# Layer 1's gate summed beside the layer's first products, and the squares of retention's output on ScalarE

## The chip, the cores and the metric

The kernel runs on one core of one Trainium2 chip. The metric is the device time of one execution in microseconds. Three executions of the kernel before took 675.12, 677.21 and 678.33 us; the median is 677.21. A core has TensorE (PE in the profile, its weight loads PEld), VectorE (DVE), ScalarE (ACT), GpSimd (POOL) and SyncE (SP, which here issues the transfers). Each works through its own list of instructions in order; semaphores make one wait for another.

## The reference

A trunk of two layers on 512 tokens of width 1024, in float32. In each layer

```
mod = silu(c) @ w_ada[l] + b_ada[l];  shift, scale, gate = split(mod, 3)
h = rms_norm(x, norm_g[l]) * (1 + scale) + shift
proj = h @ w_in[l]                  # 1024 x 3712: q, k, v, gate of A, B and C
A: differential attention, 4 heads   B: dilated window attention, 6 heads x 3 patterns
C: retention in both directions, 4 heads, values of 96, then rms_norm over the 96
y = concat([oa, ob, oc] * silu of their gates) @ w_out[l]
x = x + gate * y
```

The gate is a row of 1024 numbers that is wanted only where x is updated, at the end of the layer. shift and scale are wanted at its start.

## The kernel before

Tokens lie in four tiles of 128 partitions (t = 0 to 3). Each float32 product is made of three matmuls on values split into a high and a low part: high by high, high by low, low by high (`products`, L322 to L333). A weight block is a `Piece`: SP loads 2 x 128 rows of it into one of the five buffers `raw`, ScalarE writes the high part (whi, wsp or wrow), VectorE or, for each third piece, GpSimd the low part (L302). A buffer of raw is free when both have read it.

The work of a layer is a list of groups of matmuls. `at(g, fn)` hangs a piece of other work on the number g of a group, and `issue` emits the groups in order, each followed by what hangs on it. A scheduler of the framework then orders each engine's instructions by its own estimates and places the waits. So the number in `at` sets roughly where work stands in each engine's list, and the emitted order of each engine is fixed before the run.

The layer boundary: at the end of layer 0 the output products of the second 512 columns run, token tile by token tile. For each tile VectorE forms y (L1112, product by gate) and x (L1117), ScalarE the sum of squares of x (junk), VectorE and GpSimd the factor of the norm (rstd, L1084, L569, L199) and the modulated tiles hn (`h_tile`; VectorE multiplies, GpSimd adds at L565), TensorE transposes four of them (L554), ScalarE writes the high part hT and VectorE the low part hL (L559). Right behind layer 0's output products TensorE begins layer 1's V columns, tile by tile, which need hT and hL of that tile, and then the Q columns.

The gate: `ada_steps` (L440 to L466) sums a half of it, 512 columns, in four steps. Each loads two rows of w_ada per partition, 512 KB, into a raw buffer, and adds them with two vector instructions (L459, through the helper at L159) into the accumulator ada_acc, one of two buffers that GpSimd clears and SP fills with the bias. Its end is a matmul with ones and a copy by ScalarE. `plan_ada` (L1070) hangs loads, additions and end on groups: a load six groups ahead of its additions, a step every four groups. Both halves are hung relative to g_gb, the group at which the last columns of B start: additions at g_gb - 55 and g_gb - 31 onward, ends at g_gb - 18 and g_gb - 17. In layer 1, g_gb is 128 groups behind g_v, the first group of V.

Retention C: `att` forms the scores, `chunk` (L952) sums inner and cross part of a token tile in PSUM, ScalarE copies them to cno, GpSimd squares them into csq (L960), VectorE sums the squares (css, L962), `rms_end` ends with a power on GpSimd (L199). `norm` (five groups later) multiplies on VectorE and GpSimd, `gate_done` comes later. csq lies in the pool "e" of five buffers, which the scores use too.

Of the kernel before, what the change touches and what calls it, by code (L numbers as in the profile page):

```python
# [9 lines left out]
F32 = mybir.dt.float32  # L10
F32R = mybir.dt.float32r
AF = mybir.ActivationFunctionType
OP = mybir.AluOpType
AX = mybir.AxisListType
PSUM = bass.MemoryType.PSUM

D = 1024
S = 512
L = 2
P = 128  # L20
# [5 lines left out]
H_C, DK_C, DV_C = 4, 48, 96  # L26
# [14 lines left out]
MODS = 12  # L41
H_0, H_1 = 8, 9
C_GAP, C_DECAY, C_TURN, C_STATE = 3, 4, 4, 7
C_ATT, C_PAIR, C_OUT, C_STEP, C_NORM = 8, 3, 13, 2, 7
GATE, GATE_GAP, GATE_END = 55, 24, 18
GB_OUT, PIECE_0, PIECE_M = 9, 2, 3              
SETUP, TABLES, RET_T, TAB1 = 12, 12, 19, 9      
N_A1, N_B1, N_SOFT = 5, 5, 9
# [81 lines left out]
def dram(ap, offset, dims):  # L130
    return bass.AP(tensor=ap.tensor, offset=ap.offset + offset, ap=[list(d) for d in dims])
# [3 lines left out]
def encoder(ctx, tc, x, c, norm_g, w_ada, b_ada, w_in, w_out, params, consts, out):  # L135
# [8 lines left out]
    ep = pool("ep", 5)  # L144
# [7 lines left out]
    V, A, G, T = nc.vector, nc.scalar, nc.gpsimd, nc.tensor  # L152
    dma = nc.sync.dma_start

    def act(o, i, f=AF.Copy, **kw):
        A.activation(o, i, f, **kw)  # L156

    def stt(o, a, s, b, op0, op1):
        V.scalar_tensor_tensor(o, a, s, b, op0, op1)  # L159
# [4 lines left out]
    def at(g, fn, *args):  # L164
        plan.setdefault(g, []).append((fn, args))
# [139 lines left out]
    def rows2(raw, w, first, row, pair, step, cnt, n):  # L305

        if cnt == 1:
            dma(raw[:, :, :n], dram(w, first, [[row, P], [pair, 2], [1, n]]))
            return
        for i in range(2):  # L310
            dma(raw[:, i, :cnt * n].rearrange("p (j n) -> p j n", j=cnt), dram(w, first + i * pair, [[row, P], [step, cnt], [1, n]]))
# [26 lines left out]
    def tok_(t):  # L338
        return slice(t * P, (t + 1) * P)
# [100 lines left out]
    def ada_steps(l, cols, use):  # L440

        (c0, n), cnt = cols[0], len(cols)
        step = cols[1][0] - c0 if cnt > 1 else 0
        z = {}

        def load(r):
            def fn():
                raw = z[r] = rp.tile([P, 2, 512], F32, name="raw")
                rows2(raw, w_ada, l * D * 3 * D + r * 3 * D + c0, KD * 3 * D, 3 * D, step, cnt, n)
                if r == 0:  # L450
                    a = z["a"] = two.tile([P, 512], F32, name="ada_acc")
                    G.memset(a, 0.0)
                    dma(a[0:1].rearrange("o (j n) -> o j n", j=cnt), dram(b_ada, l * 3 * D + c0, [[0, 1], [step, cnt], [1, n]]))
            return fn

        def add(r):
            def fn():
                for rr in range(2):
                    stt(z["a"], z[r][:, rr], cs[:, r + rr:r + rr + 1], z["a"], OP.mult, OP.add)  # L459
            return fn  # L460

        def end():
            ps = sc_p.tile([P, 512], F32, name="ada_ps", tag="sc")
            T.matmul(ps, ones, z["a"], start=True, stop=True)  # L464
            use(ps)
        return [load(r) for r in range(0, KD, 2)], [add(r) for r in range(0, KD, 2)], end  # L466
# [101 lines left out]
    def rms_end(s, n, width):  # L568
        V.tensor_scalar(s, s, 1.0 / width, EPS, OP.mult, OP.add)  # L569
        pow_half(s, s, n)  # L570
# [261 lines left out]
    class Retention:  # L832
# [41 lines left out]
        def qk_done(self, t, ps, g0):  # L874
            if t == 0:
                self.raw = {}
            raw = self.raw[t] = ep.tile([P, 8, DK_C], F32, name="craw", tag="e")
            act(raw.rearrange("p h n -> p (h n)"), ps[:, :384])
            g = g0 + 12 + C_GAP * t
            at(g + 1, self.rope, t)  # L880
            at(g + C_DECAY, self.decay, t)
            at(g + C_TURN, self.turn_qk, t)
            at(g + C_TURN + 1, self.turn_f, t)
            at(g + C_STATE, self.state, t)
            if t == NT - 1:
                at(g + C_ATT, self.back)
                for h in range(0, H_C, 2):
                    at(g + C_ATT + C_PAIR * h // 2, self.att, h)
                for n in range(NT):
                    at(g + C_OUT + C_STEP * n, self.chunk, n)  # L890
                    at(g + C_OUT + C_NORM + C_STEP * n, self.norm, n)

        def rope(self, t):
# [45 lines left out]

        def att(self, h):  # L940
            if h == 0:
                self.atts, self.o, self.ss = {}, {}, {}

            ps = [sc_p.tile([P, NT, P], F32, name="catt", tag="sc") for _ in range(2)]
            for n in range(NT):
                for j, r in enumerate((F_, B_)):
                    T.matmul(ps[j][:, n], self.qkT[r, 2 + h // 2, tok_(n)], self.qkT[r, h // 2, tok_(n)], start=True, stop=True)
            for j in range(2):
                at_ = self.atts[h + j] = ep.tile([P, NT, P], F32, name="att", tag="e")
                V.tensor_tensor(at_, ps[j], self.dcm[:, h + j].unsqueeze(1).to_broadcast([P, NT, P]), OP.mult)  # L950

        def chunk(self, n):  # L952
            ps = pv_p.tile([P, H_C, DV_C], F32, name="co", tag="pv")
            for h in range(H_C):
                T.matmul(ps[:, h], self.atts[h][:, n], self.vc[n][:, h], start=True, stop=False)
                T.matmul(ps[:, h], self.qfT[:, h, tok_(n)], self.st[n][:, h], start=False, stop=True)
            o = self.o[n] = one.tile([P, H_C, DV_C], F32, name=f"cno{n}", tag=f"s{4 + n}")
            act(o, ps)
            sq = ep.tile([P, H_C, DV_C], F32, name="csq", tag="e")
            G.tensor_tensor(sq, o, o, OP.mult)  # L960
            ss = self.ss[n] = sm.tile([P, H_C], F32, name="css")
            V.tensor_reduce(ss, sq, AX.X, OP.add)  # L962
            rms_end(ss, H_C, DV_C)

        def norm(self, n):
# [19 lines left out]
    def layer(l):  # L985
# [3 lines left out]
        if l:  # L989
            g_v, _ = in_chunk(l, [(COL_VC, 384)], ret.v_done, first=True)  # L990
# [36 lines left out]
        g_gb = len(groups)  # L1027
# [36 lines left out]
        def gate_use(hf):  # L1064
            def use(ps):
                z[hf] = two.tile([P, 512], F32, name="gate", tag="ga")
                act(z[hf], ps)
            return use

        def plan_ada(steps, g, gap, g_end=0):  # L1070
            loads, adds, end = steps
            for i in range(4):
                at(g + gap * i - 6, loads[i])
                at(g + gap * i, adds[i])
            at(max(g + gap * 4, g_end), end)
            return g + gap * 4

        for hf in range(2):
            plan_ada(ada_steps(l, [(2 * D + hf * 512, 512)], gate_use(hf)), g_gb - GATE + GATE_GAP * hf, 4, g_gb - GATE_END + hf)


        def h_stats(t):
# [15 lines left out]
        for hf in range(2):  # L1098
# [59 lines left out]
            for j, t in turns:  # L1158
# [9 lines left out]
                g = len(groups) - 1  # L1168
# [9 lines left out]
        if not last:  # L1178
            g = g_gb - MODS
            for q in range(4):  # L1180
                g = plan_ada(mod_steps(l + 1, q), g, 3)
# [76 lines left out]
    for l in range(1, L):  # L1258
        layer(l)
# [35 lines left out]
```

## Time and profile before

| | us |
|---|---|
| median of three runs | 677.21 |
| the profiled execution | 676.71 |
| its span | 674.9 |
| TensorE busy | 630.2 (93%) |
| VectorE busy | 501.0 (74%) |
| ScalarE busy | 330.4 (49%) |
| GpSimd busy | 261.4 (39%) |

The span runs from the first to the last recorded instruction of the core. Busy time is the time in which an engine executes; weight loads are counted apart from matmuls and overlap them. A time in brackets behind an instruction is the idle time of its engine ahead of it, with the work that ended it. Layer 0 ends, and layer 1 begins, at about 355 us. Layer 1's V columns end at about 380, its C part runs from about 430, its two attentions from about 460 to 600, its output products in the last 75 us.

### The profile page before, as it was taken

The numbers are of one execution on the slowest core, as the hardware profiler recorded it, in microseconds if no ns is written. First come the engines' busy times: TensorE is split into PE (matmuls) and PEld (weight loads), VectorE is DVE, ScalarE is ACT, GpSimd is POOL, SyncE is SP. The second block draws the span as 40 slices with busy tenths as digits, with TensorE's granted clock in tenths as the row PEclk, the third lists the DMA queues.
The fourth block names the chain that finished last, engine by engine and source line by source line (L and its number), as shares of the span: only waits on it lengthen the run. The fifth ranks groups of instructions, "written<-read, shape, count | busy, mean of one in ns | idle before, by whom it ended". The sixth has DMA issues, their size and how long they took to land.

```text
span 674.9 us, 10503 instructions
## 1 busy us (share of the span) xinstructions
PE 630.2 (93%) x3487; PEld 516.0 (76%) x3487; DVE 501.0 (74%) x1157; ACT 330.4 (49%) x722; POOL 261.4 (39%) x252
## 2 busy tenths in 40 slices
PE   6889998999999996999998999989999999989997
PEld 2778787977887784677776998887778887767786
DVE  1998697589988988897769154768997888576443
ACT  5534352447655674554423243434757476656410
POOL 3427363666343520211457252767052613121200
PEclk9789998999999999899999999999999999999999
DMA  9796133344555556575643122235454625423211
GB/s 316 250 335 159 57 94 97 105 120 120 148 127 173 144 165 170 166 243 181 216 166 119 32 83 75 64 84 155 114 156 119 193 85 161 116 64 133 93 63 63
DMA packets 87134, 93.20 MB, mean 138 GB/s; under 512 B 7044, under 2 KB 68004, under 8 KB 87080
## 3 DMA queue, kind: packets, MB, share of 16 engines
q1 hardware_dynamic: 87080, 92.53, 45.6%
q8 instruction: 28, 0.46, 0.3%
q14 instruction: 26, 0.21, 0.1%
HBM read 72.58 MB, written 4.19 MB: 114 GB/s over the span
## 4 chain that ended last, share of the span: by engine, by line
PE 41%; DVE 8%; POOL 4%; issue 2%; ACT 2%; DMA 0%; POOLq 0%; ACTq 0%; DVEq 0%; SPq 0%
PE acc L333 8%; PE acc L332 8%; PE acc L331 8%; PE tr L554 5%; PE pv L703 3%; PE acc L327 1%; PE acc L329 1%; PE acc L328 1%; DVE wlo L302 1%; PE sc L726 1%; PE sc L787 1%; DVE ada_acc L159 1%; PE sc L788 1%; DVE pt L693 1%; PE ada_ps L464 1%
## 5 line engine op out<-in xcount | busy, mean ns | idle before, releaser
L331 PE MATMUL acc<-whi,hT 128*128 128x384 f32 (+1 forms) x424 | 155.4, 366 | 1.5 <-ACT vc L156 1.0
L333 PE MATMUL acc<-whi,hL 128*128 128x384 f32 (+1 forms) x424 | 153.2, 361 | 0.0
L332 PE MATMUL acc<-wlo,hT 128*128 128x384 f32 (+1 forms) x424 | 152.7, 360 | 0.0
L302 POOL TENSOR_TENSOR wlo<-raw,whi 128x768 fp32r<-128x768 f32 (+1 forms) x26 | 55.1, 2119 | 126.4 <-ACT whi L156 119.2
L156 ACT ACTIVATE whi<-raw 128x768 fp32r<-128x768 f32 (+1 forms) x75 | 69.6, 929 | 52.9 <-PE acc L333 41.6
L331 PEld LDWEIGHTS acc<-whi,hT 128*128 128x128 f32 x424 | 80.2, 189 | 8.5 <-ACT vc L156 1.4
L302 DVE TENSOR_TENSOR wlo<-raw,whi 128x384 fp32r<-128x384 f32 (+1 forms) x98 | 64.1, 683 | 28.6 <-ACT whi L156 28.3
L333 PEld LDWEIGHTS acc<-whi,hL 128*128 128x128 f32 x424 | 80.1, 189 | 6.2
L332 PEld LDWEIGHTS acc<-wlo,hT 128*128 128x128 f32 x424 | 80.2, 189 | 5.7
L159 DVE SCALAR_TENSOR_TENSOR ada_acc<-raw,cs,ada_acc 128x512 f32<-128x512 f32 x86 | 72.3, 845 | 5.3 <-DMA raw<-in_w_ada_dram 2.7
L199 POOL TENSOR_TENSOR qkss<-qkss,nhalf 128x4 f32<-128x4 f32 (+1 forms) x40 | 54.1, 1352 | 49.2 <-DVE qkss L569 48.2
L156 ACT ACTIVATE e<-sc,mx 128x512 f32<-128x512 f32 x64 | 43.9, 688 | 37.7 <-DVE mx L728 23.3
L728 DVE TENSOR_REDUCE mx<-sc 128x1 f32<-128x512 f32 x64 | 43.1, 684 | 9.9 <-PE sc L726 9.6
L156 ACT ACTIVATE sb<-sb,mx 128x512 f32<-128x512 f32 x48 | 34.5, 719 | 29.1 <-DVE mx L792 27.9
L703 PE MATMUL pv<-pt,v 128*64 128x256 f32 x320 | 38.9, 385 | 3.8 <-DVE pt L693 3.8
L693 DVE COPY pt<-tr 128x512 f32<-128x512 f32 x40 | 27.4, 686 | 15.7 <-PE tr L554 15.6
L156 ACT ACTIVATE pt<-tr 128x512 f32<-128x512 f32 x40 | 23.8, 596 | 29.1 <-PE tr L554 29.0
L554 PE MATMUL tr<-cst,sb 128*128 128x128 f32 x192 | 30.9, 284 | 6.4 <-DVE nat L159 2.4
L703 PEld LDWEIGHTS pv<-pt,v 128*64 128x64 f32 x320 | 21.2, 136 | 19.1 <-DVE pt L693 8.4
L554 PEld LDWEIGHTS tr<-cst,sb 128*128 128x128 f32 x192 | 22.0, 142 | 17.2 <-ACT pt L156 8.1
L792 DVE CUSTOM_DVE_ANT_0 sb<-sc,cst 128x512 f32<-128x512 f32 x48 | 32.0, 682 | 3.8 <-PE sc L788 3.0
L624 POOL TENSOR_TENSOR qkn<-qkraw,qkss 128x256 f32<-128x256 f32 x40 | 28.9, 722 | 5.0 <-DVE ga L620 2.0
(298 smaller groups left out, 1433.1 us busy)
## 6 DMA issues: line engine op xcount, KB each, us to landing
raw<-in_w_ada_dram SPq DMA_DIRECT2D x64, 256.0 KB, 4.0
raw<-in_w_in_dram SPq DMA_DIRECT2D x48, 192.0 KB, 2.7
raw<-in_w_in_dram SPq DMA_DIRECT2D x24, 384.0 KB, 3.5
raw<-in_w_in_dram SPq DMA_DIRECT2D x32, 256.0 KB, 3.5
raw<-in_w_ada_dram SPq DMA_DIRECT2D x16, 512.0 KB, 4.6
raw<-in_w_out_dram SPq DMA_DIRECT2D x32, 256.0 KB, 3.2
x<-in_x_dram SPq DMA_DIRECT2D x8, 512.0 KB, 3.4
stB<-nat SPq DMA_DIRECT2D x32, 128.0 KB, 2.4
```

Of the source, the lines that this page charges most:

```text
L156: A.activation(o, i, f, **kw)
L159: V.scalar_tensor_tensor(o, a, s, b, op0, op1)
L199: G.tensor_tensor(o, i, nhalf[:, :n], OP.pow)
L302: (G if pool else V).tensor_tensor(l2[:, z], r2[:, z], h2[:, z].bitcast(F32), OP.subtract)
L331: T.matmul(ps, ah, hi[i], start=s_, stop=False)
L332: T.matmul(ps, ah, lo[i], start=False, stop=False)
L333: T.matmul(ps, al, hi[i], start=False, stop=e_)
L554: T.transpose(ps[:, i, :], b, ident)
L693: V.tensor_copy(pt, ps)
L703: T.matmul(self.pv[h * 64:h * 64 + 64, i * 256:i * 256 + 256], self.u.v[:, k, h * 64:h * 64 + 64], self.pt[h][:, k], start=k == 0, stop=k ...
L728: V.tensor_reduce(mx, ps, AX.X, OP.max, negate=True)
L792: V.tensor_tensor_reduce(sb, ps, cst[:, m0:m0 + S], 1.0, 3e38, OP.add, OP.min, mx)
```

## The change

Two things. In layer 1 the gate's loads and additions hang on groups g_v + 8 and g_v + 24 onward (GATE_1, GATE_GAP_1), its loads six groups earlier each; its end stays where it was, and layer 0 stays as it was. And the squares of C's output are a ScalarE activation (Square) in both layers, while the sum of squares and what follows from it is a step of its own, `sums`, one group after `chunk`.

```diff
--- before.py
+++ after.py
@@ -41,8 +41,9 @@
 MODS = 12
 H_0, H_1 = 8, 9
 C_GAP, C_DECAY, C_TURN, C_STATE = 3, 4, 4, 7
-C_ATT, C_PAIR, C_OUT, C_STEP, C_NORM = 8, 3, 13, 2, 7
+C_ATT, C_PAIR, C_OUT, C_STEP, C_SUMS, C_NORM = 8, 3, 13, 2, 1, 7
 GATE, GATE_GAP, GATE_END = 55, 24, 18
+GATE_1, GATE_GAP_1 = 8, 16
 GB_OUT, PIECE_0, PIECE_M = 9, 2, 3              
 SETUP, TABLES, RET_T, TAB1 = 12, 12, 19, 9      
 N_A1, N_B1, N_SOFT = 5, 5, 9
@@ -888,6 +889,7 @@
                     at(g + C_ATT + C_PAIR * h // 2, self.att, h)
                 for n in range(NT):
                     at(g + C_OUT + C_STEP * n, self.chunk, n)
+                    at(g + C_OUT + C_SUMS + C_STEP * n, self.sums, n)
                     at(g + C_OUT + C_NORM + C_STEP * n, self.norm, n)
 
         def rope(self, t):
@@ -939,7 +941,7 @@
 
         def att(self, h):
             if h == 0:
-                self.atts, self.o, self.ss = {}, {}, {}
+                self.atts, self.o, self.sq, self.ss = {}, {}, {}, {}
 
             ps = [sc_p.tile([P, NT, P], F32, name="catt", tag="sc") for _ in range(2)]
             for n in range(NT):
@@ -956,10 +958,12 @@
                 T.matmul(ps[:, h], self.qfT[:, h, tok_(n)], self.st[n][:, h], start=False, stop=True)
             o = self.o[n] = one.tile([P, H_C, DV_C], F32, name=f"cno{n}", tag=f"s{4 + n}")
             act(o, ps)
-            sq = ep.tile([P, H_C, DV_C], F32, name="csq", tag="e")
-            G.tensor_tensor(sq, o, o, OP.mult)
+            sq = self.sq[n] = ep.tile([P, H_C, DV_C], F32, name="csq", tag="e")
+            act(sq, o, AF.Square)
+
+        def sums(self, n):
             ss = self.ss[n] = sm.tile([P, H_C], F32, name="css")
-            V.tensor_reduce(ss, sq, AX.X, OP.add)
+            V.tensor_reduce(ss, self.sq[n], AX.X, OP.add)
             rms_end(ss, H_C, DV_C)
 
         def norm(self, n):
@@ -1076,7 +1080,8 @@
             return g + gap * 4
 
         for hf in range(2):
-            plan_ada(ada_steps(l, [(2 * D + hf * 512, 512)], gate_use(hf)), g_gb - GATE + GATE_GAP * hf, 4, g_gb - GATE_END + hf)
+            g = g_v + GATE_1 + GATE_GAP_1 * hf if l else g_gb - GATE + GATE_GAP * hf
+            plan_ada(ada_steps(l, [(2 * D + hf * 512, 512)], gate_use(hf)), g, 4, g_gb - GATE_END + hf)
 
 
         def h_stats(t):
```

On VectorE, at the layer boundary, these rows stand in the order before. y and x belong to the second half of layer 0's output (x_3444 is token tile 0), wrow is the low part of a block of V weights, hn are layer 1's normed columns.

```order
L1112 TENSOR_TENSOR y<-acc,gate 128x512
L302 TENSOR_TENSOR wrow<-raw,wrow 128x384 x2
L1112 TENSOR_TENSOR y<-acc,gate 128x512
L1117 TENSOR_TENSOR x_3444<-y,x_3444 128x512
L1084 TENSOR_TENSOR rstd<-part 128x1
L569 TENSOR_SCALAR rstd<-rstd 128x1
L159 SCALAR_TENSOR_TENSOR hn<-x_3444,rstd,mod_3188 128x256
L159 SCALAR_TENSOR_TENSOR hn<-x_3444,rstd,mod_3436 128x256
L159 SCALAR_TENSOR_TENSOR hn<-x_3444,rstd,mod_3650 128x256
```

And after:

```order
L1117 TENSOR_TENSOR y<-acc,gate 128x512
L160 SCALAR_TENSOR_TENSOR ada_acc<-raw,cs,ada_acc 128x512
L303 TENSOR_TENSOR wrow<-raw,wrow 128x384 x2
L160 SCALAR_TENSOR_TENSOR ada_acc<-raw,cs,ada_acc 128x512 x5
L1117 TENSOR_TENSOR y<-acc,gate 128x512
L1122 TENSOR_TENSOR x_3444<-y,x_3444 128x512
L160 SCALAR_TENSOR_TENSOR ada_acc<-raw,cs,ada_acc 128x512
L1089 TENSOR_TENSOR rstd<-part 128x1
L160 SCALAR_TENSOR_TENSOR ada_acc<-raw,cs,ada_acc 128x512
L570 TENSOR_SCALAR rstd<-rstd 128x1
L160 SCALAR_TENSOR_TENSOR mod_3791<-ada_ps,ng 128x256
L160 SCALAR_TENSOR_TENSOR hn<-x_3444,rstd,mod_3188 128x256
```

The gate's additions (ada_acc) have moved in between; six of the first eight stand ahead of this y, and two between x and the norm's factor.

SP's queue at the same place before, with numbered names: raw_3754 to raw_3798 are blocks of V weights, raw_4019 to raw_4165 those of Q, far is x on its way out of the core.

```order
L308 DMA raw_3775<-in_w_in_dram 128x2x384
L453 DMA ada_acc_5092<-in_b_ada_dram 1x512
L308 DMA raw_3798<-in_w_in_dram 128x2x384
L308 DMA raw_4019<-in_w_in_dram 128x2x384
L308 DMA raw_4078<-in_w_in_dram 128x2x384
L308 DMA raw_4131<-in_w_in_dram 128x2x384
L308 DMA raw_4165<-in_w_in_dram 128x2x384
L311 DMA raw_4230<-in_w_in_dram 128x4x128 x2
L1177 DMA far0_97<-x0_3444 128x1024
```

And after:

```order
L309 DMA raw_3775<-in_w_in_dram 128x2x384
L454 DMA ada_acc_3964<-in_b_ada_dram 1x512
L309 DMA raw_3798<-in_w_in_dram 128x2x384
L309 DMA raw_3962<-in_w_ada_dram 128x2x512
L309 DMA raw_4024<-in_w_in_dram 128x2x384
L309 DMA raw_4032<-in_w_ada_dram 128x2x512
L309 DMA raw_4087<-in_w_in_dram 128x2x384
L309 DMA raw_4115<-in_w_ada_dram 128x2x512
L309 DMA raw_4144<-in_w_in_dram 128x2x384
L309 DMA raw_4152<-in_w_ada_dram 128x2x512
L309 DMA raw_4182<-in_w_in_dram 128x2x384
L1182 DMA far0_97<-x0_3444 128x1024
```

Each load of Q weights (raw_4024, raw_4087, raw_4144, raw_4182) now has a load of w_ada ahead of it and one behind it.

On TensorE, in the tail of layer 1, the last transposes (tr) of the probabilities sb, the scores sc and the sums pv of B before, and the products that stand right ahead of them.

```order
L331 MATMUL acc<-whi,hT 128x384
L332 MATMUL acc<-wlo,hT 128x384
L333 MATMUL acc<-whi,hL 128x384
L554 MATMUL tr<-cst,sb 128x128 x8
L787 MATMUL sc<-stB,stC 128x512
L788 MATMUL sc<-stB,stC 128x512
L703 MATMUL pv<-pt,v 64x256 x8
L554 MATMUL tr<-cst,sb 128x128 x4
L787 MATMUL sc<-stk,stq 128x512
L788 MATMUL sc<-stk,stq 128x512
L554 MATMUL tr<-cst,sb 128x128 x4
L554 MATMUL tr<-cst,oat 128x128 x4
```

And after:

```order
L555 MATMUL tr<-cst,sb 128x128 x4
L332 MATMUL acc<-whi,hT 128x384
L333 MATMUL acc<-wlo,hT 128x384
L334 MATMUL acc<-whi,hL 128x384
L332 MATMUL acc<-whi,hT 128x384
L555 MATMUL tr<-cst,sb 128x128 x4
L788 MATMUL sc<-stB,stC 128x512
L789 MATMUL sc<-stB,stC 128x512
L333 MATMUL acc<-wlo,hT 128x384
L334 MATMUL acc<-whi,hL 128x384
L332 MATMUL acc<-whi,hT 128x384
L704 MATMUL pv<-pt,v 64x256 x8
```

Products (acc) of a weight block that stood ahead of the first transposes stand between them now. Line numbers after the change are one to five higher.

## Rows read from the trace of the kernel before

**Rows 1.** Busy time of the page: engine, us, share of the span, instructions.
```profile
PE 630.2 (93%) x3487; PEld 516.0 (76%) x3487; DVE 501.0 (74%) x1157; ACT 330.4 (49%) x722; POOL 261.4 (39%) x252
```

**Rows 2.** Windows: start:end, length, busy us (instructions) of each engine, granted clock, DMA.
```profile
380.00:430.00 50.00, 49.78 (x290) 44.11 (x291) 25.57 (x58) 19.25 (x39) 19.39 (x14) 1.00 0.26 74
430.00:460.00 30.00, 27.11 (x181) 26.14 (x178) 18.68 (x40) 9.24 (x19) 21.61 (x19) 1.00 0.29 78
460.00:560.00 100.00, 95.80 (x542) 79.20 (x542) 88.48 (x232) 63.55 (x161) 42.35 (x38) 1.00 0.51 142
560.00:615.00 55.00, 51.50 (x302) 38.53 (x300) 37.24 (x93) 34.26 (x70) 8.65 (x8) 1.00 0.36 104
580.00:600.00 20.00, 16.50 (x102) 11.27 (x101) 12.10 (x34) 11.24 (x25) 5.32 (x4) 1.00 0.49 132
```

**Rows 3.** Tile ada_acc, its vector additions: count, ns min/median/max, first and last start.
```profile
L159 DVE SCALAR_TENSOR_TENSOR ada_acc<-raw,cs,ada_acc x86: 701/748/2465, 9.4 to 540.3; 128x512 f32<-128x512 f32 x86
```

**Rows 4.** Windows, the layer boundary, columns as in rows 2.
```profile
341.00:355.00 14.00, 14.00 (x62) 10.98 (x61) 8.61 (x17) 4.39 (x10) 6.86 (x8) 1.00 0.52 185
```

**Rows 5.** Timeline, SP's issues (start, us, count behind x).
```profile
331.24 0.37 SPq L308 DMA_DIRECT2D raw<-in_w_in_dram  x1
338.64 0.37 SPq L308 DMA_DIRECT2D raw<-in_w_in_dram  x1
```

**Rows 6.** DMA issues of the page: count, KB each, us to landing.
```profile
raw<-in_w_ada_dram SPq DMA_DIRECT2D x16, 512.0 KB, 4.6
raw<-in_w_in_dram SPq DMA_DIRECT2D x24, 384.0 KB, 3.5
```

**Rows 7.** Timeline, VectorE at the boundary: start, us, what, idle before and releaser.
```profile
330.63 0.54 DVE L302 TENSOR_TENSOR wsp<-raw,wsp 128x384 fp32r<-128x384 f32 x1
337.44 3.70 DVE L302 TENSOR_TENSOR wrow<-raw,wrow 128x384 fp32r<-128x384 f32 x2 [3.03 <-ACT wrow L156]
341.78 0.69 DVE L1112 TENSOR_TENSOR y<-acc,gate 128x512 f32<-128x512 f32 x1 [0.64 <-PE acc L333]
357.00 0.68 DVE L559 TENSOR_TENSOR hL<-tr,hT 128x512 fp32r<-128x512 f32 x1
```

**Rows 8.** Timeline, TensorE at the boundary.
```profile
357.83 0.63 PE L554 MATMUL tr<-cst,hn 128*128 128x128 f32 x4 [1.84 <-DVE hL L559]
```

**Rows 9.** Timeline of TensorE, and windows, after another pause.
```profile
111.97 0.63 PE L554 MATMUL tr<-cst,qkn 128*128 128x128 f32 x4 [2.79 <-DVE nat L159]
...
114.00:116.00 2.00, 2.00 (x15) 1.78 (x13) 1.50 (x4) 0.14 (x1) 0.00 (x0) 0.50 0.24 69
```

**Rows 10.** Timelines of ScalarE, POOL, VectorE and TensorE around csq in layer 1.
```profile
434.73 0.49 ACT L156 ACTIVATE cno<-co 128x384 f32<-128x384 f32 x1 [3.71 <-PE co L956]
...
437.45 0.83 POOL L960 TENSOR_TENSOR csq<-cno 128x384 f32<-128x384 f32 x1
...
438.31 0.55 DVE L962 TENSOR_REDUCE css<-csq 128x4 f32<-128x384 f32 x1 [4.14 <-POOL csq L960]
...
443.02 0.63 PE L554 MATMUL tr<-cst,qkn 128*128 128x128 f32 x4 [2.89 <-DVE nat L159]
```

**Rows 11.** Timeline, POOL at the boundary.
```profile
336.20 4.53 POOL L302 TENSOR_TENSOR wlo<-raw,whi 128x1024 fp32r<-128x1024 f32 x2
...
345.58 1.80 POOL L565 TENSOR_TENSOR hn<-hn,mod 128x256 f32<-128x256 f32 x2 [0.60 <-DVE hn L159]
```

**Rows 12.** Tile csq (as rows 3); waits: engine, releaser, us, times, longest.
```profile
L960 POOL TENSOR_TENSOR csq<-cno x8: 827/829/1272, 120.6 to 454.4; 128x384 f32<-128x384 f32 x8
...
DVE css L962 <- POOL csq L960: 10.5, 5, 4.1
```

**Rows 13.** Timelines of VectorE and TensorE around one addition.
```profile
499.04 0.74 DVE L159 SCALAR_TENSOR_TENSOR ada_acc<-raw,cs,ada_acc 128x512 f32<-128x512 f32 x1
...
500.43 1.30 PE L703 MATMUL pv<-pt,v 128*64 128x256 f32 x10 [1.64 <-DVE pt L693]
```

**Rows 14.** Timeline, TensorE in the tail.
```profile
591.58 0.66 PE L554 MATMUL tr<-cst,oat 128*128 128x128 f32 x4 [0.78 <-DVE pt L693]
```

## The prediction

> **What bounds the kernel.** I read the busy times first: TensorE works 630.2 us of a span of 674.9, VectorE 501.0 [rows 1]. So there are about 45 us in all in which TensorE has nothing to do, and an edit counts only by what it does to those gaps. The windows of the stages come next, to see where the gaps lie: 2.9 us of 30 in 430 to 460, 4.2 of 100 in 460 to 560, 3.5 of 55 in 560 to 615 [rows 2]. VectorE is 88% busy in 460 to 560, so a vector instruction taken out there can be felt, and one put into a stretch where VectorE has pauses can be free. The profiled execution took 676.71 us, 1.81 more than its span and 0.5 below the median 677.21; I sum against 676.71.
>
> The change has two edits, and they act at four places.
>
> **1. The gate's sums at the layer boundary: a loss.** In layer 1 sixteen vector additions (16 of the 86 in [rows 3], median 0.748 us) and eight 512 KB loads move from 446 to 541 us forward to the end of layer 0's output products. Nothing is added in number: 16 x 0.748 = 12.0 us of VectorE change place. The program's order for VectorE shows all eight additions of the first half, and two of the second, ahead of the first hL, the low part of layer 1's first activations. In the trace VectorE is busy 8.61 us of the 14 from 341 to 355 [rows 4], so it has 5.4 us of pauses there. Ten additions are 7.5 us: even if they filled all the pauses 2.1 us would stick out. They don't, because they wait for their loads:
> - The order for SP puts a load of the gate behind each load of weights. The five buffers of raw are shared, so a load is issued when its buffer is free. Before, the first and the third of the Q weights were issued at 331.24 and 338.64 [rows 5], each when its buffer came free. Now the first gate load takes the buffer of the first (331.2), the second gate load that of the third (338.6); the third goes as soon as the first one's two additions are done (about 342), the fourth when the second one's are.
> - A load of this size lands 4.6 us after its issue [rows 6]. So: first at 335.8 (its first addition falls in the pause of 3.03 us ahead of 337.44 [rows 7]), second at 343.2, third at 346.5, fourth at 349.3.
> - In VectorE's order six additions, three loads' worth, stand before the y that ran at 341.78 [rows 7]. The third load's two end at 346.5 + 1.5 = 348.0, so this y is 6.2 us late. The fourth load's first addition stands between x and rstd, at about 349.4. After that the old pauses give some back: hn of the first token tile comes at about 352, the third tile's y, with two more additions before it, some 6.5 late as well, and the first hL at about 361.5 instead of 357.00 [rows 7]: +4.5.
> - TensorE's output products need nothing of this; then it waited 1.84 us for that hL, to 357.83 [rows 8]. It now waits about 6.3. Of the remaining additions of the second half one or two stand among the later tiles' hL and I add 0.2. Term: +4.7 us.
> Bounds: +2.1 from below (ten additions less all the pauses), +8 from above: loads of 6 us each instead of 4.6 (two landings in a row on the path, +2.8), plus three quarters of a us for a later addition. I take 4.7 since it is built from the median landing. Behind it I see nothing else that waits: VectorE is busy 25.57 us of the 50 from 380 on [rows 2], so what is left of the additions finds room. The end of the gate (the matmul with ones) stays where it was; its two accumulators are only held longer.
>
> A stall of 6 us could also cost clock. TensorE started at 111.97 after a pause of 2.79 us, and in 114 to 116 the granted clock is 0.50, the lower level of 1.2 GHz [rows 9]; the pause of 2.89 us ahead of 443.02 [rows 10] is followed by no such stretch, the mean of 430 to 460 is 1.00 [rows 2]. Where it falls here it is for some 3.4 us, half of which is lost: 1.7 us. I keep that for the range. "TensorE: Matmul & The Clock Gate" of the Trainium skill (HAM oscillation) says that a wait which idles TensorE makes the next stretch start cold, paid anew each time. By that rule the sum would be 1.7 higher; the trace has it both ways, so I leave it out of the sum.
>
> The same place holds a second risk. wrow at 337.44 took 3.70 us for two instructions, where one of that size took 0.54 at 330.63 [rows 7]; POOL ran two wlo beside it, 4.53 us from 336.20 [rows 11]. The additions will stand beside POOL's hn in the same way [rows 11], and the longest of the 86 took 2.465 us [rows 3]. "SBUF — State Buffer" (SBUF: two separate sides) of the Trainium skill gives the reason: VectorE with two SBUF inputs and a GpSimd instruction that reads SBUF take one port pair in turn, for whole instructions. The rows agree. By it two of the additions would each lose one POOL instruction, 0.9 us (half of 1.80), and the sum would be 1.8 higher.
>
> **2. Squares of C off POOL: a gain in layer 1.** Eight POOL multiplications of 0.829 us go [rows 12]; ScalarE gets eight activations, each as long as the cno copy of the same shape, 0.49 [rows 10], 3.9 us in all on an engine that is busy 9.24 of 30 us there [rows 2]. VectorE waited 10.5 us in five goes for csq, 4.1 the longest [rows 12]. That one ends at 438.31: cno was copied at 434.73, but POOL worked on norms of Q and K and began csq at 437.45, css followed at 438.31, then the power on POOL, the norm, and two wlo with a nat behind each; the nat released the transposes at 443.02 after TensorE's 2.89 us [rows 10]. With csq on ScalarE at 435.2, css runs at 435.75 and POOL takes the power right after its last qkn, at 437.5, where it waited for csq and css until about 439.1, so the norm runs 1.6 earlier; the two wlo and nat behind it follow, and the stall shrinks by about 1.4. In layer 0 VectorE's waits for csq stop nobody on TensorE. Term: -1.4; bounds 0 (the two wlo wait for their own whi, nothing moves) and -2.9 (the whole stall); above zero by 0.5 if a square delays a ScalarE copy that TensorE waits for.
>
> **3. The additions gone from 446 to 541: a gain.** VectorE is 11.5 us short of full there and TensorE 4.2 us [rows 2]. The clearest case: an addition at 499.04 (0.74 us) stands before a pt copy, and pv waited 1.64 us for that copy [rows 13]; without it some 0.66 less. Nearly every other wait of TensorE in this window ends on a vector or softmax instruction. 12 us less of 88 would shorten most of those: I take half of TensorE's idle time, -2.0; bounds 0 and -4.2.
>
> **4. The order of products in the tail.** The scheduler, with those additions out of its list, spreads nine triples of products among the transposes and scores at 584 to 595, where before they had run ahead of them in one block. TensorE had no products there and idled between transposes, as ahead of 591.58 for a pt copy [rows 14]; in 580 to 600 it is idle 3.5 us [rows 2]. 27 products of some 0.18 us, 4.8 us of work, would fill such holes. But the transposes then come earlier and may wait for a softmax that isn't ready. I take two thirds of the idle time, since the products are spread over all the holes: -2.3; bounds 0 and -3.5.
>
> **Sum.** 4.7 - 1.4 - 2.0 - 2.3 = -1.0: 676.71 - 1.0 = 675.7 us.
>
> **Rivals.**
> - *The boundary swallows the additions* (faster). If the loads land early, in 3.5 us as smaller ones do [rows 6], the boundary costs its lower bound 2.1, and with VectorE lighter the two later gains come to -3.5 each: 2.1 - 1.4 - 3.5 - 3.5 = -6.3, 670.4. For it: VectorE's 5.4 us of pauses. Against: the buffers, which chain the third and fourth load to the additions of the first two.
> - *The boundary stall decides* (slower). VectorE, in order, holds y behind a load; TensorE stands still 8 us or more and starts cold. 7 + 1.7 - 1.4 - 1 - 0.5 = +5.8: 682.5. It decides from the point where the boundary costs more than the gains bring plus 3.4: 9.1 us with my gains, 6.3 with half of them. For it: the chained loads, the long two-input instructions beside POOL. Against: the 4.2 and 3.5 us of idle TensorE late in the kernel that are there to win.
> - *Neither reaches the end* (no change). TensorE is 96% busy in 460 to 560 and the products of the tail have to run somewhere; then terms 3 and 4 are near zero, and with a boundary of 3 and csq at -1.4 it is +1.6: 678.3.
>
> **Chances.** What a measurement of this kernel can tell from no change is about 0.5%, 3.4 us: below 673.8 is faster, above 680.6 slower. My forecast 0.26 and the third rival 0.16 lie within it, 0.42. The first rival and what lies near it has 0.34, the second 0.24. The range reaches from 669.5 to 681.8: beyond the first rival's value and just short of the second's; the forecast's own range is 673 to 679.5.
>
> **What would show it.** Right: VectorE waits for w_ada loads between 341 and 350, the first hL about 361, a TensorE stall of about 6 us before the first transposes of layer 1; then css without a wait for csq, the stall at 443 about halved, TensorE over 96 of 100 us between that layer's V and the output, and fewer holes before the last products. Wrong: hL not later than 358 (term 1 falls, the first rival holds), a stall over 9 us or a granted clock of 0.5 behind it (the second), or as much TensorE idle time late in the kernel as before (terms 3 and 4 fall).

## The result, and the profile after

The change makes the kernel slower. Ten runs have a median of 681.27 us against 677.59 for ten runs of before; the ratio is 1.006, with an interval of 1.0041 to 1.0079. That is 4.1 us more (2.8 to 5.4), where 1.0 us less was forecast. The page after (span; then busy time of each engine):

```profile
span 678.2 us, 10493 instructions
PE 634.1 (93%) x3487; PEld 518.9 (77%) x3487; DVE 507.6 (75%) x1157; ACT 334.9 (49%) x730; POOL 253.2 (37%) x244
```

TensorE is busier than in [rows 1], though it computes the same: matmuls at half clock count as busy for longer.

**The boundary.** SP's issues of the gate's first four loads (start, duration) stand at the places that the order showed:

```profile
332.50 0.37 SPq L309 DMA_DIRECT2D raw<-in_w_ada_dram  x1
340.34 0.37 SPq L309 DMA_DIRECT2D raw<-in_w_ada_dram  x1
343.54 0.37 SPq L309 DMA_DIRECT2D raw<-in_w_ada_dram  x1
346.52 0.37 SPq L309 DMA_DIRECT2D raw<-in_w_ada_dram  x1
```

VectorE after (start, duration, what, in brackets the idle time before and what ended it), for [rows 7]: the additions wait for these loads, the y of the first token tile follows at 349.02 instead of 341.78, the x of the third tile takes 2.10 us, and the first hL stands at 364.52 instead of 357.00.

```profile
336.23 1.82 DVE L160 SCALAR_TENSOR_TENSOR ada_acc<-raw,cs,ada_acc 128x512 f32<-128x512 f32 x1 [0.55 <-DMA raw<-in_w_ada_dram]
344.96 1.54 DVE L160 SCALAR_TENSOR_TENSOR ada_acc<-raw,cs,ada_acc 128x512 f32<-128x512 f32 x2 [1.44 <-DMA raw<-in_w_ada_dram]
347.56 1.54 DVE L160 SCALAR_TENSOR_TENSOR ada_acc<-raw,cs,ada_acc 128x512 f32<-128x512 f32 x2 [1.07 <-DMA raw<-in_w_ada_dram]
349.02 0.68 DVE L1117 TENSOR_TENSOR y<-acc,gate 128x512 f32<-128x512 f32 x1
350.95 0.75 DVE L160 SCALAR_TENSOR_TENSOR ada_acc<-raw,cs,ada_acc 128x512 f32<-128x512 f32 x1 [0.53 <-DMA raw<-in_w_ada_dram]
359.69 2.10 DVE L1122 TENSOR_TENSOR x<-y,x 128x512 f32<-128x512 f32 x1
364.52 0.68 DVE L560 TENSOR_TENSOR hL<-tr,hT 128x512 fp32r<-128x512 f32 x1
```

GpSimd's instruction beside that x:

```profile
359.45 1.80 POOL L303 TENSOR_TENSOR wlo<-raw,whi 128x768 fp32r<-128x768 f32 x1
```

ScalarE: the square of the third tile's x (junk) waits for it, and the first hT stands behind that square.

```profile
361.83 0.63 ACT L157 ACTIVATE junk<-x 128x512 f32<-128x512 f32 x1 [4.03 <-DVE x L1122]
363.19 0.58 ACT L157 ACTIVATE hT<-tr 128x512 fp32r<-128x512 f32 x1
```

TensorE waits first for that hT and then for the hL, 6.24 and 0.52 us, where it waited 1.84 [rows 8]:

```profile
363.82 0.69 PE L332 MATMUL acc<-wsp,hT 128*128 128x384 f32 x1 [6.24 <-ACT hT L157]
365.35 1.09 PE L555 MATMUL tr<-cst,hn 128*128 128x128 f32 x4 [0.52 <-DVE hL L560]
```

Windows in and behind the stall (start:end, length, busy us of PE, PEld, DVE, ACT, POOL, granted clock, DMA share, GB/s): the clock falls to 0.50, 1.2 GHz, within the stall, at about 359.6, and is back at about 369.8. TensorE works again in the last six of these ten us.

```profile
358.00:360.00 2.00, 0.00 (x0) 0.00 (x0) 1.97 (x3) 0.00 (x0) 2.00 (x3) 0.90 0.19 78
360.00:362.00 2.00, 0.00 (x0) 0.00 (x0) 1.79 (x1) 0.17 (x1) 1.60 (x2) 0.50 0.86 246
366.00:368.00 2.00, 2.00 (x9) 2.00 (x8) 1.96 (x4) 1.32 (x3) 1.41 (x2) 0.50 0.21 76
368.00:370.00 2.00, 2.00 (x9) 1.90 (x8) 0.78 (x4) 0.00 (x0) 1.49 (x2) 0.54 0.96 324
370.00:372.00 2.00, 2.00 (x14) 1.79 (x13) 1.42 (x3) 0.60 (x1) 0.74 (x1) 1.00 0.81 235
```

**Behind it.** The squares are on ScalarE, for [rows 12], and VectorE's waits for them fell from 10.5 to 5.6 us:

```profile
L157 ACT ACTIVATE csq<-cno x8: 514/525/527, 121.0 to 458.8; 128x384 f32<-128x384 f32 x8
...
DVE css L966 <- ACT csq L157: 5.6, 4, 1.7
```

In layer 1 css waits 1.72 instead of 4.14 us, and TensorE 1.45 instead of 2.89 [rows 10]:

```profile
445.18 0.55 DVE L966 TENSOR_REDUCE css<-csq 128x4 f32<-128x384 f32 x1 [1.72 <-ACT csq L157]
...
450.88 0.63 PE L555 MATMUL tr<-cst,qkn 128*128 128x128 f32 x4 [1.45 <-DVE nat L160]
```

The late windows, for [rows 2] (they begin at the same times, though TensorE arrives later): TensorE idles 1.8 us of 100 instead of 4.2, 2.4 of 55 instead of 3.5, and 1.2 instead of 3.5 in 580 to 600.

```profile
460.00:560.00 100.00, 98.20 (x558) 82.44 (x556) 79.24 (x216) 65.69 (x167) 42.75 (x39) 1.00 0.39 104
560.00:615.00 55.00, 52.59 (x305) 39.72 (x305) 40.54 (x100) 33.01 (x69) 11.09 (x9) 1.00 0.36 103
580.00:600.00 20.00, 18.76 (x114) 14.75 (x113) 12.89 (x32) 10.82 (x22) 3.10 (x3) 1.00 0.53 145
```

One of the two waits that I had named stayed: the pv of [rows 13] still waits 1.54 us, with no addition right ahead of its pt copy. The other, of the transposes in the tail [rows 14], is gone; two longer ones have come, 1.10 us ahead of 570.30 for a pt copy and 0.92 us ahead of 599.14 for VectorE's cth.

```profile
504.86 1.95 PE L704 MATMUL pv<-pt,v 128*64 128x256 f32 x16 [1.54 <-DVE pt L694]
```

**One measure for all kernels.** Two matmuls mark the boundary in every trace: the first output product on o, 311.89 before, and the first product on Q's weights, 379.83 before. After:

```profile
313.15 0.39 PE L332 MATMUL acc<-whi,o 128*128 128x512 f32 x1
...
389.12 0.34 PE L332 MATMUL acc<-whi,hT 128*128 128x384 f32 x1
```

They are 75.97 us apart instead of 67.94: the boundary costs 8.03. From the second mark to the last matmul it is 285.54 instead of 291.50, 5.96 less. Both together are +2.1; the other 1.26 of the profile's difference lie ahead of the first mark, where the kernels of this study differ by -0.5 to +2.9 without a pattern that goes with their edits. A part of it goes with the granted clock: the five kernels with 17 us at 0.50 up to the first mark, before among them, lie at -0.5 to +1.3, the others, with 20 to 24 us, at +0.3 to +2.9. Between +2.1 and the lower end of the timed 2.8 to 5.4 some 0.7 us stay unexplained.

From the end of layer 0's output products to the second mark TensorE does the same work in both kernels. Windows of that stretch, before and after:

```profile
355.64:379.83 24.19, 20.96 (x126) 19.05 (x124) 18.15 (x37) 7.64 (x14) 13.85 (x18) 1.00 0.26 79
357.57:389.12 31.55, 23.54 (x125) 21.59 (x125) 25.36 (x48) 9.93 (x19) 17.88 (x22) 0.84 0.42 133
```

It is busy 2.6 us longer and idle 4.8 us longer; the output products ahead of it take 0.7 us longer. So of the 8.03 at most some 2.6 us are the half clock's, and fewer where TensorE would have waited for hL instead.

### The profile page after: what moved, and what is told of

The parts are those of the page before. It is cut to its first block, busy times and chain, and to the rows that moved or that the text cites. A ratio compares the mean times of both kernels' runs of the same rounds, so it can differ in the third digit from the quotient of the medians.

```text
span 678.2 us, 10493 instructions
## 1 busy us (share of the span) xinstructions
PE 634.1 (93%) x3487; PEld 518.9 (77%) x3487; DVE 507.6 (75%) x1157; ACT 334.9 (49%) x730; POOL 253.2 (37%) x244
## 4 chain that ended last, share of the span: by engine, by line
PE 38%; DVE 11%; issue 4%; POOL 3%; DMA 1%; ACT 1%; POOLq 0%; DVEq 0%; ACTq 0%
PE acc L334 8%; PE acc L332 8%; PE acc L333 7%; PE tr L555 4%; PE pv L704 3%; DVE ada_acc L160 2%; DMA raw<-in_w_ada_dram 1%; PE sc L727 1%; PE acc L328 1%; PE acc L329 1%; PE acc L330 1%; DVE hn L160 1%; PE sc L788 1%; DVE wlo L303 1%; PE sc L789 1%
## 5 line engine op out<-in xcount | busy, mean ns | idle before, releaser
L303 DVE TENSOR_TENSOR wlo<-raw,whi 128x384 fp32r<-128x384 f32 (+1 forms) x98 | 65.8, 698 | 25.1 <-ACT whi L157 25.1
L200 POOL TENSOR_TENSOR qkss<-qkss,nhalf 128x4 f32<-128x4 f32 (+1 forms) x40 | 52.3, 1308 | 48.4 <-DVE qkss L570 47.6
L727 PE MATMUL sc<-stk,stq 96*128 96x512 f32 x64 | 27.7, 440 | 2.9 <-ACT e L157 1.6
```

The lines of the kernel that those rows point to most:

```text
L200: G.tensor_tensor(o, i, nhalf[:, :n], OP.pow)
L303: (G if pool else V).tensor_tensor(l2[:, z], r2[:, z], h2[:, z].bitcast(F32), OP.subtract)
L727: T.matmul(ps, self.u.stq[0:96, m, tok_(qt)], self.u.stk[0:96, m], start=True, stop=True)
```

## The experiments

All are compared with before on the same chip. "Boundary" and "behind" are the two differences just defined, in us, from each kernel's profile; "first hL" is its start less that of before (357.00) and less the shift at the first mark.

| kernel | median | ratio, interval | boundary | behind | first hL |
|---|---|---|---|---|---|
| the change | 681.27 | 1.006 (1.0041 to 1.0079) | +8.03 | -5.96 | +6.3 |
| e1, gate only | 682.17 | 1.007 (1.0044 to 1.0096) | +6.97 | -3.47 | +6.1 |
| e2, squares only | 673.69 | 0.9952 (0.9932 to 0.9972) | -0.05 | -3.95 | |
| e3, gate at 32 | 677.01 | 0.9997 (0.9981 to 1.0013) | +0.31 | -1.20 | |
| e4, no loads | 677.90 | 1.0007 (0.9991 to 1.0023) | +5.59 | -6.33 | +5.0 |
| e5, short additions | 677.06 | 0.9998 (0.998 to 1.0017) | +4.85 | -6.19 | +3.9 |
| e6, half the gate | 679.28 | 1.0032 (1.0011 to 1.0053) | +5.21 | -2.99 | +3.6 |
| e7, half, no loads | 679.23 | 1.0039 (1.0018 to 1.0059) | +5.25 | -2.87 | +3.6 |
| e8, loads, no additions | 672.47 | 0.9923 (0.9901 to 0.9944) | +0.47 | -5.92 | 0.0 |
| e10, order of a square | 679.26 | 1.002 (0.9999 to 1.0041) | +6.39 | -5.99 | +5.2 |
| e11, first half at 28 | 675.31 | 0.9966 (0.9945 to 0.9987) | +0.59 | -3.01 | |
| e12, two places | 674.16 | 0.9946 (0.9925 to 0.9966) | +0.59 | -5.75 | |
| e13, busy TensorE | 681.41 | 1.0055 (1.0033 to 1.0078) | +6.60 | -3.38 | +3.5 |
| e14, Q block on VectorE | 677.22 | 1.0001 (0.9984 to 1.0019) | +6.27 | -6.07 | +4.5 |

**Which edit.** e1 is the kernel before with the gate's new place only; e2 the change with the old place:

```diff
-            g = g_v + GATE_1 + GATE_GAP_1 * hf if l else g_gb - GATE + GATE_GAP * hf
+            g = g_gb - GATE + GATE_GAP * hf
```

> Only the gate's move; the squares stay on GpSimd. Theory A (the additions hold y and hL back while they wait for their loads, the boundary costs about 7.9 us, and the late part gives 4.5 back): TensorE stalls about 6 us before layer 1's V, 3.9 us slower than before, about 681.5. Rival (the squares on ScalarE, not the gate, make it slower): within 1 us of before, no stall over 3 us at the boundary.

> Only the squares on ScalarE and the separate sums; the gate stays late. Theory A: layer 1's stall behind the norm's squares shrinks by 1.4 us, layer 0 loses about 0.9 us to an exp that stands behind on ScalarE: 0.5 us faster than before, about 677. Rival: 3 us slower or more, about 681.

The gate's move alone makes the kernel slower, the squares alone make it faster, by 3.2 us (1.9 to 4.6 by the interval): more than the 0.5 that I expected. The loss of 0.9 in layer 0 isn't seen (e2's first mark stands 0.25 later). In e2 VectorE and TensorE at the same place as [rows 10]:

```profile
436.54 0.55 DVE L966 TENSOR_REDUCE css<-csq 128x4 f32<-128x384 f32 x1 [1.72 <-ACT csq L157]
...
441.49 0.63 PE L555 MATMUL tr<-cst,qkn 128*128 128x128 f32 x4 [0.69 <-DVE nat L160]
```

TensorE's 2.89 us became 0.69, and two later waits (0.56 us for v ahead of 461.63 and 0.92 us for the first softmax ahead of 471.70 before) are gone as well: 1.7 us of the gain lie up to 458, 2.2 between 458 and 488. e2 beats both kernels.

**Another place for the gate.**

```diff
-GATE_1, GATE_GAP_1 = 8, 16
+GATE_1, GATE_GAP_1 = 32, 16
```

> The whole change, but the gate hung 24 groups later (GATE_1 32), behind the V columns, where VectorE has room. Theory A: no boundary loss, the stall there about 2 us as before; squares and the late part keep their gain of some 5 us: 672.5. Rival B (the late gain of 4.5 us came only because TensorE arrived 8 us later and found its inputs ready): 676 to 677.5. Rival C (the additions cost TensorE as much wherever in the first stretch they stand): 680.

The time lies in rival B's range, but not for its reason; theories A and C missed. The boundary is free again (+0.31), and the late part gains; but between 397 and 430 (on the scale of before) TensorE lost 3.8 us, since the additions now stand among VectorE's work for C's decayed keys and queries, one of them for 2.86 us, and TensorE's transposes wait for that. (Rival B's reason falls with e8 and e12 below: there TensorE passes the second mark only some 0.5 us late, and the late gain is nearly that of the whole change.) In e3:

```profile
403.52 2.86 DVE L160 SCALAR_TENSOR_TENSOR ada_acc<-raw,cs,ada_acc 128x512 f32<-128x512 f32 x1
...
424.10 0.63 PE L555 MATMUL tr<-cst,qfb 128*128 128x128 f32 x4 [1.09 <-DVE qfb L907]
```

**Waits or work at the boundary.** e4 leaves out layer 1's gate loads (the additions read a resident tile); e5 keeps loads and waits but sums 16 columns of 512; e6 moves the first half alone; e7 is e6 without that half's loads; e8 is the change without the additions.

```diff
+                if l and c0 >= 2 * D:  # e4; e7: c0 == 2 * D
+                    z[r] = cst[:, :512].unsqueeze(1).to_broadcast([P, 2, 512])
+                else:
...
+                m = 16 if l and c0 >= 2 * D else 512  # e5
...
-                    stt(z["a"], z[r][:, rr], cs[:, r + rr:r + rr + 1], z["a"], OP.mult, OP.add)
+                    stt(z["a"][:, :m], z[r][:, rr, :m], cs[:, r + rr:r + rr + 1], z["a"][:, :m], OP.mult, OP.add)  # e5
...
+                for rr in range(0 if l and c0 >= 2 * D else 2):  # e8
...
+            g = g_v + GATE_1 if l and not hf else g_gb - GATE + GATE_GAP * hf  # e6, e7
```

> The whole change, but layer 1's gate is summed from a resident tile: its eight loads of w_ada are left out, so layer 1's gate isn't the reference's; the sixteen additions stay about where they were. Theory A (it is the wait for the loads): the boundary costs 2 to 3 us instead of 7.9, first hL about 359 to 360 on the scale of before, 676. Rival C (the additions' own time and their sharing with GpSimd): boundary 6 us or more, 680.

Theory A fell here: without any wait for a load the boundary still costs 5.6, just under what theory C asked. It is not a clean test, since the scheduler put fourteen additions ahead of the first hL, so the next four followed.

> The whole change with all its loads and waits, but layer 1's gate additions sum 16 of the 512 columns, so layer 1's gate isn't the reference's; ten of them stand ahead of the first hL as in the change. Theory A2 (the waits for the loads hold y): the boundary still costs 5 us or more, y of the first tile at 347 to 348. Theory C2 (the additions' own time, some of it beside GpSimd, fills VectorE): the boundary costs under 2.5 us, total about 675.

> Only the first half of the gate moves; the second half stays late. Eight additions with their waits ahead of the first hL instead of ten. Theory A2: the two additions that go are not waited for, the boundary costs 6.5 to 7.5 us. Theory C2: 1.5 us less and one stretch beside GpSimd less, 5 to 6 us. Total 677 to 679.

> As the half gate, but its eight additions read a resident tile and its four loads are left out, so that half of layer 1's gate isn't the reference's. Against the half gate it takes away the waits alone. Theory A2: the boundary falls to 1.5 us or less. Theory C2: it stays over 3 us.

> The whole change with layer 1's sixteen gate additions left out (its gate is the bias alone) and all eight loads kept where the change puts them. Theories A2 and C2: the boundary costs less than 0.7 us, and the rest of the gain stays: about 672. Rival (the loads delay the Q weights or their traffic the others): 2 us or more behind the V columns.

The loads alone cost 0.47: in e8 TensorE's stall is that of before, and in the stretch up to the second mark it is busy 21.10 us, nearly as before (20.96), at a clock of 1.00.

```profile
357.58:382.23 24.65, 21.10 (x124) 19.07 (x124) 18.24 (x37) 7.65 (x14) 13.84 (x18) 1.00 0.45 152
...
359.77 0.63 PE L555 MATMUL tr<-cst,hn 128*128 128x128 f32 x4 [1.84 <-DVE hL L560]
```

With the waits and hardly any of the additions' own time (e5, ten additions) the boundary costs 4.85, against theory C2 and just under A2's 5; with the additions' time and no wait (e7, eight additions) 5.25, against A2; with both (e6, eight) 5.21. Either of the two is enough and they don't add up: while an addition waits for its load, the work behind it on VectorE waits too, and without the wait VectorE spends that time adding, part of it beside GpSimd. Neither takes away one thing alone, though. With the edit the scheduler also changed the order: e7 has all eight additions ahead of the first tile's y, where e6 has six, and e5 and e7 have two and three of them ahead of the two wrow, beside GpSimd, where the change and e6 have one. How much of e7's 5.25 is that order isn't shown. In e5:

```profile
337.91 3.62 DVE L160 SCALAR_TENSOR_TENSOR ada_acc<-raw,cs,ada_acc 128x16 f32<-128x16 f32 x2 [0.59 <-DMA raw<-in_w_ada_dram]
345.99 0.50 DVE L160 SCALAR_TENSOR_TENSOR ada_acc<-raw,cs,ada_acc 128x16 f32<-128x16 f32 x2 [1.86 <-DMA raw<-in_w_ada_dram]
348.71 0.68 DVE L1118 TENSOR_TENSOR y<-acc,gate 128x512 f32<-128x512 f32 x1
357.83 0.23 DVE L160 SCALAR_TENSOR_TENSOR ada_acc<-raw,cs,ada_acc 128x16 f32<-128x16 f32 x1
363.81 0.68 DVE L561 TENSOR_TENSOR hL<-tr,hT 128x512 fp32r<-128x512 f32 x1
```

The waits hold the y to 348.71, 345.8 on the scale of before. In e7, with no wait in the way, three additions take 5.71 us beside GpSimd's x and wlo, the other five follow the two wrow, and y comes at 346.65, 346.4 on that scale:

```profile
334.62 5.71 DVE L160 SCALAR_TENSOR_TENSOR ada_acc<-cst,cs,ada_acc 128x512 f32<-128x512 f32 x3
342.83 3.90 DVE L160 SCALAR_TENSOR_TENSOR ada_acc<-cst,cs,ada_acc 128x512 f32<-128x512 f32 x5
346.65 0.69 DVE L1120 TENSOR_TENSOR y<-acc,gate 128x512 f32<-128x512 f32 x1
360.87 0.68 DVE L563 TENSOR_TENSOR hL<-tr,hT 128x512 fp32r<-128x512 f32 x1
```

**What makes the first hL still later in the change.** e10 hangs the third tile's sum of squares three groups later, so that ScalarE writes the first hT ahead of it. e14 lets VectorE make the low part of the first Q block, the wlo of GpSimd beside which x took 2.10 us:

```diff
-                        at(g + (2 if hf == 0 else 1), part_sum, t, cols, hf)  # e10
+                        dz = 3 if hf and t == 2 else 0
+                        at(g + (2 if hf == 0 else 1) + dz, part_sum, t, cols, hf)  # h_stats too
...
-            g_qk, _ = in_chunk(l, [(COL_QC, 384)], ret.qk_done)  # e14
+            g_qk, qp = in_chunk(l, [(COL_QC, 384)], ret.qk_done)
+            qp[0].dve = True
...
```

> The whole change, with the sum of squares of the third token tile hung three groups later, so that ScalarE writes the first hT ahead of it. Theory E (ScalarE's order holds hT behind the late third tile): the first hL comes 1 to 2 us earlier, the boundary costs 6 to 7 us instead of 8. Rival (VectorE's own order holds hL): no difference over 0.5 us.

> The whole change, with the low part of the first Q block made by VectorE instead of GpSimd. It takes away the GpSimd instruction beside which the third tile's x took 2.10 us. Theory F (the shared port adds to the boundary): x of the third tile takes 0.7 us, hT and the first hL come 0.7 to 1.5 us earlier, boundary about 7 us instead of 8. Rival (VectorE pays the same in its own instructions): within 0.4 us.

Both theories hold. e10 came as E said: hL 1.1 us earlier, 1.6 us less at the boundary. e14 gave more than F's 0.7 to 1.5: hL and the boundary 1.8 us less. Timed, e14 is some 4 us faster than the change, twice what its trace shows; the rest isn't explained. In e14 the x takes 0.69, and hL stands at 363.28, which is 361.5 on the scale of before:

```profile
360.35 0.69 DVE L1123 TENSOR_TENSOR x<-y,x 128x512 f32<-128x512 f32 x1
363.28 0.68 DVE L560 TENSOR_TENSOR hL<-tr,hT 128x512 fp32r<-128x512 f32 x1
```

**The half clock.** e9 and e13 are e7 with extra matmuls behind layer 0's output products.

```diff
+                    if not last and hf and (j, t) == (6, NT - 1):
+                        warm = sc_p.tile([P, 512], F32, name="warm", tag="sc")
+                        for _ in range(4):  # e9: 8
+                            T.matmul(warm[:, :512], ones, cst[:, :512], start=True, stop=True)
```

> As the half gate without loads (its half of layer 1's gate isn't the reference's), with eight extra matmuls on resident tiles behind layer 0's output products, so that TensorE works through most of its stall of about 4 us; first hL where it was. Theory D (a good part of the boundary's cost is the half clock behind the stall): the granted clock stays at 1.00 there and layer 1's V ends 1.5 to 3 us earlier than without the extra matmuls, boundary 2.5 to 3.7 instead of 5.25. Rival (the clock costs nothing, V is paced by hL): boundary 4.7 or more.

e9 tells nothing of the price: its eight matmuls were sixteen instructions of 7.03 us, longer than the stall, and by a slip in the edit they also ran behind the first half of the output (689.16 us, ratio 1.016, boundary +13.65). e13 mends both.

> The half gate without loads (its half of layer 1's gate isn't the reference's) with four extra matmuls on resident tiles, some 3.5 us, only behind layer 0's last output products, so that TensorE works in the 3.6 us in which it stood still. Theory D: the granted clock stays at 1.00 behind it and the boundary costs 2.5 to 4 us instead of 5.25. Rival (V is paced by hL, the clock costs nothing): 5 us or more.

In e13 the extra matmuls ran for 3.59 us and the clock stayed at 1.00 behind them. But the first hL was as late as in e7, TensorE then waited 1.69 us for it and 1.90 for GpSimd's hn, and the clock fell after those, in 368 to 370:

```profile
360.00:362.00 2.00, 0.98 (x3) 0.15 (x1) 2.00 (x6) 1.08 (x2) 1.45 (x2) 1.00 0.95 283
368.00:370.00 2.00, 2.00 (x8) 2.00 (x7) 1.14 (x4) 0.56 (x1) 0.39 (x1) 0.50 0.49 151
...
357.38 3.59 PE L1119 MATMUL warm<-cst,ones 128*128 128x512 f32 x8
367.30 0.63 PE L558 MATMUL tr<-cst,hn 128*128 128x128 f32 x4 [1.90 <-POOL hn L569]
```

The boundary got no cheaper, 6.60: later hn and hL made TensorE wait again. But VectorE's order behind the first hL is another in e13, and the clock fell there too, so e13 doesn't price the half clock. What the traces allow is a bound and a trend. The same work kept TensorE busy 2.6 us longer in the change than before, and in e8, at full clock, 0.1 longer. And the boundary exceeds the lateness of hL by 0.5 in e8, by 0.6 in e4, which had some 3.0 us at 0.50 behind its first hL, by 0.9 in e1 (3.4 us), and by 1.7 to 1.8 in the change, e6, e7 and e14 (5.3 to 5.8 us). e13, with another order, lies outside with 3.1.

**Better places.** e11 puts the first half at g_v + 28, e12 the second at g_gb + 6 as well:

```diff
+            g = (g_v + 28, g_gb + 6)[hf] if l else g_gb - GATE + GATE_GAP * hf  # e12
```

> Squares on ScalarE, the gate's first half hung at g_v + 28, behind the V columns; the second half late as before. With the boundary and C's decays out of the way, half the late gain of 2 us on top of the squares' alone: 0.5 to 1 us faster than those, about 673. Rival (the eight additions collide with C's preparation as sixteen did): 675.

> As e11, and the second half at g_gb + 6, beside the last columns and the first output products, where VectorE is about 60 percent busy. All sixteen additions leave 446 to 541: 1 to 2 us faster than the squares alone, about 672. Rival (the additions hold the last softmax or the first outputs there): 674 or more.

e11 is no better than the squares alone. Its trace had gained about 4.4 us by 590 and lost 1.4 of that by 600 (both on the scale of before), with the clock at 0.50 from 592 to 595; e2 has the same four pauses of TensorE just ahead of that (0.22, 0.79, 0.69 and 0.31 us) and kept 1.00. The window 592 to 594, e11 first, then e2:

```profile
592.00:594.00 2.00, 2.00 (x7) 1.58 (x7) 1.92 (x6) 0.73 (x2) 0.00 (x0) 0.50 0.44 154
592.00:594.00 2.00, 2.00 (x14) 1.28 (x14) 2.00 (x6) 0.00 (x0) 1.20 (x1) 1.00 0.00 0
```

e6, e7 and e13, which also move the first half alone, have such a fall at 595 to 597. e12's parts sum to -5.2, its time to 0.9946 (0.9925 to 0.9966) of before, which cannot be told from e2's 0.9952; 674.16 us is what its rival allowed. So the gate may as well stay where it was.

## Why the prediction was wrong

Term 1 has the wrong size and turned the sign. Term 2, and terms 3 and 4 together, have wrong sizes too, but these two errors cancel, by luck.

- *Term 1, the boundary, +4.7: measured +8.03.* This is the step that failed: the way from y to the first hL, and what follows behind that hL. The path up to y was right, load by load: y was forecast at 348.0 and came at 349.02 less the shift of 1.26, so 347.8. The first hL was forecast at 361.5 and came at 363.3 on that scale. The missing 1.8 is the risk that I had priced at 1.8 and left out of the sum, with another victim than the additions: x of the third tile beside GpSimd's wlo. That the two amounts agree is luck. e14 takes out that meeting and has its hL at 361.5. I did not see that ScalarE's hT stands behind the square of that tile, which passes the delay on (e10: 1.6 us). Behind the first hL I added 0.2 us; measured is 8.03 - 6.25, 1.8. The half clock lies there, for some ten us and not the 3.4 that I had kept for the range, and the trend above speaks for it; it isn't proved, since no kernel changes the clock alone. The stall of 6.24 us equals the 6.3 forecast only by luck: hL came later than forecast, but the output products, of which I had said that they need nothing of the additions, also ended 0.7 us later, and TensorE then stood a second time, 0.52 us.
- *Its cause.* I blamed the loads' waits, and called ten additions less the pauses a lower bound of 2.1. e7 has eight additions, no waits, and 5.25: the pauses aren't usable, because additions placed ahead of y hold up a chain (y, x, square, rstd, hn) whose pauses come between its own steps. (Its order is not e6's, as said above.)
- *Term 2, the squares, -1.4: -3.95 alone.* The 2.89 us stall shrank to 1.45 in the change, as forecast, and to 0.69 in e2; the waits behind it, for v and the first softmax, I had not counted, though they stood in the trace. css without a wait for csq, which I named as a sign, did not come: 1.72 us are left.
- *Terms 3 and 4, the additions gone, -4.3: -3.47 alone (e1) and about -2.0 on top of the squares* (5.96 less 3.95). The wait that I showed for it [rows 13] was not theirs: pv waits 1.54 us for its pt without any addition. The tail is fuller, -2.3 of idle time in 580 to 600, but not all of that reaches the end.

Terms 2 to 4 together were forecast at -5.7 and came at -5.96, so the sign was lost at the boundary alone. Of the 5.1 us between the forecast and the timed change the boundary explains 3.3; the 1.26 ahead of the first mark and the rest stay open. At the boundary it was the second rival's case, with 7 + 1.7: its place was right, its trigger, the waits, only half of it, and its late gains, 2.9 in all, were half of the measured ones.

On the shared port: "SBUF — State Buffer" of the Trainium skill (SBUF: two separate sides) says that the loser waits for whole instructions. The runs agree: in e5 two additions of 16 columns, 0.23 us each elsewhere, took 3.62 us beside GpSimd's x and wlo:

```profile
336.38 2.75 POOL L1123 TENSOR_TENSOR x<-y,x 128x512 f32<-128x512 f32 x2 [1.16 <-ACT junk L157]
339.10 4.62 POOL L303 TENSOR_TENSOR wlo<-raw,whi 128x1024 fp32r<-128x1024 f32 x2
```

## What to carry to other kernels

Idle time of an engine inside a dependent chain is not room: work hung ahead of the chain's first step delays every later one, whether it waits or computes. Before moving work to a place with pauses, follow what stands behind it on that engine, and behind those results on the others, to the engine that sets the end. And an instruction with two SBUF operands on VectorE is priced, where GpSimd works beside it, by the length of GpSimd's instruction and not by its own median.

## What was not expected of the hardware

Two 16-column additions beside GpSimd took 3.62 us (e5), about as long as the two wrow of 384 columns before, 3.70 [rows 7]: the length of the other engine's instruction sets the price, not one's own. A pause of 1.84 us ahead of layer 1's V leaves the clock at 1.00 (before, e8), while in e6 the clock falls behind a pause of 2.53 us and stays at 0.50 from 359 to 366; in e13 it fell behind pauses of 1.69 and 1.90 us, and in e11 behind four of under 0.8 us that e2 has as well, without a fall. "TensorE: Matmul & The Clock Gate" of the Trainium skill (HAM oscillation) lets an idle wait make what follows cold; the runs show it for some pauses under 3 us and not for others of the same length (2.79 us ahead of 111.97 with it, 2.89 us ahead of 443.02 without).
